# Two full seven-product sets per gate and up pair, a third running sum that stays a PSUM bank, and sums taken from turned tiles

## The chip, the cores and the metric

The kernel runs on one core of one Trainium2 chip. The metric is the device time of one execution in microseconds, the median of several runs. TensorE (PE) multiplies, VectorE (DVE) and ScalarE (ACT) prepare operands and empty PSUM, SyncE (SP) issues nearly all DMAs, GpSimd (POOL) does almost nothing here.

## What is computed

Two decoder layers on 256 rows of 2048 columns. In each layer a mixer (attention and a gated recurrence between an input and an output projection) is followed by a feed-forward part and a gate with input embeddings. The change lies in the feed-forward part and in a helper that other projections share:

```
h = rms_norm(x, pre_ffn_gain[i])
f = (silu(h @ w_ffn_gate[i]) * (h @ w_ffn_up[i])) @ w_ffn_down[i]
x = x + rms_norm(f, post_ffn_gain[i])
```

The gate and up weights are 2048 x 5632, the down weights 5632 x 2048, all fp32.

## The kernel before, in words

**Precision.** Every fp32 operand is split into two fp32r tiles, a rounded high part (a cast on ACT, line 203 or 305) and the rest (a subtraction on DVE, line 204 or 315). A product is then three matmuls: high by high, low by high, high by low.

**Tiles.** Rows come in two tiles of 128 (t = 0, 1). The inner dimension comes in chunks of 256, that is two slices k of 128. Weights come in tiles of 256 x 512 (`wr`, 512 KB, ten buffers; `wh` and `wl`, seven buffers each). One slice of one row tile against one weight tile is three matmuls of 512 columns, so a chunk costs 12 matmuls for both row tiles and one weight tile, and one split.

**strip (line 318)** multiplies all chunks plainly for one 512-column strip.

**paired (line 399)** does two strips, wa and wb, together. For two chunks it uses seven block products in place of eight (Strassen's scheme in Winograd's form, `fast`, lines 442 to 499). The left blocks are sums of row tiles (`mixed`, line 356), the right blocks sums and differences of weight tiles, made in place on DVE by `sub` (line 433), then split by `parts` (line 430). The products go into four running sums: u (first, sixth and seventh product; a bank of pool `pms`), `accc`, `acce`, `acca` (pool `pacc`, four banks). Three times u or `accc` is copied out by ACT (`saved`, line 425), and line 496 adds u to the copy of `accc` on DVE. The remaining chunks go through `plain` (line 503), wb's second row tile into a fresh bank `accd` (line 544 or 530). `second` (line 481) follows the first plain chunk of wa, `third` (line 487) follows the last. At the end of each sum, `summed` (line 392) or the caller's function adds bank and saved copy.

**Gate and up (gated, line 1178).** Eleven column strips in each layer; strip 0 goes plainly, strips 1 to 10 through `paired` with eight chunks: chunks 0 and 1 in seven products, and, by the argument `half`, chunk 2 cut into two slices of 128 and handled the same way (products of half the length; the sums from `mixed_half`, line 378). Chunks 3 to 7 are plain. Each finished strip is transposed through DRAM (`shuffled`, line 241: a DVE transpose, a store, four loads) and split into `hidden` (`split_shuffled`, line 279).

**Down.** The strips are consumed in groups of 2, 3, 3 and 3 (line 1208). Each group is multiplied with w_ffn_down, two output strips at a time, through `paired` with 4 or 6 chunks (the last group's output strips 2 and 3 plainly). The sums for this come from `mixed(first)`, over the group's first hidden strip, eight ticks into the group's last gate and up pair (line 1204).

**Order.** One counter of ticks (line 95) starts deferred steps (`later`, line 73). Engines run their own instruction lists in order; the order in a list is set by a scheduler in program order as far as its readiness estimate allows. All weight loads and all turn DMAs stand in SP's queue. `load_gain` (line 547) loads a broadcast gain row into one of two `gB` buffers.

Of the 40 calls of `paired` in the two layers, 4 belong to w_out, 20 to gate and up, 14 to down, 2 to the embedding gate (these with `after`).

Of the kernel before, what the change touches and what calls it, by code (L numbers as in the profile page):

```python
# [47 lines left out]
def decoder(ctx: ExitStack, tc: tile.TileContext, x, p, positions, w_in, attn_sinks,  # L48
# [307 lines left out]
    def mixed(lhs, tags=None):  # L356

        if tags:
# [19 lines left out]
    def mixed_half(x):  # L378

        hi = sp.tile([P, 4, 1, P], F32R, tag="ax", name="sum")  # L380
        lo = sp.tile([P, 4, 1, P], F32R, tag="ay", name="sum")
        full = nat((P, 2, SEQ))
        V.tensor_tensor(full, x[0][:, 0:2].bitcast(F32), x[1][:, 0:2].bitcast(F32), op=ALU.add)
        a11, a21, a12, a22 = (full[:, k, t * P:(t + 1) * P] for k in range(2) for t in range(NT))
        s = nat((P, 4, 1, P))
        for i, p, q, op in ((0, a21, a22, ALU.add), (1, s[:, 0, 0], a11, ALU.subtract),
                            (2, a11, a21, ALU.subtract), (3, a12, s[:, 1, 0], ALU.subtract)):
            V.tensor_tensor(s[:, i, 0], p, q, op=op)
        split(s, hi, lo)
        return lambda i: lambda k: (hi[:, i - 1, 0], lo[:, i - 1, 0])  # L390
# [8 lines left out]
    def paired(lhs, sums, wa, wb, cols, done_a, done_b, nch=8, row0=0, skews=(0, 0),  # L399
               after=None, mixed_order=False, half=None):  # L400
# [35 lines left out]
        def split_one(r, k):  # L436
            hi = wps.tile([P, 2, W], F32R, tag="wh", name="wh")
            lo = wps.tile([P, 2, W], F32R, tag="wl", name="wl")
            split(r[:, k], hi[:, k], lo[:, k])
            return hi, lo  # L440

        def fast():
            mix = sums()
            r11, r12 = fetch_w(wa, base, cols[0]), fetch_w(wb, base, cols[1])
            if half:
                more = half()
                g, p = fetch_w(wa, base + 2, cols[0]), fetch_w(wb, base + 2, cols[1])
            r21, r22 = fetch_w(wa, base + 1, cols[0]), fetch_w(wb, base + 1, cols[1])
            u = bank()
            acc(u, block(0, 0), parts(r11))  # L450
            if half:
                gx = parts(g)
                acc(u, block(2, 0), gx, (0,))
            x = [saved(u)]
            sub(r11, r12, r11)
            c = psum("accc")
            acc(c, mix(1), parts(r11))
            if half:
                sub(g[:, 0], p[:, 0], g[:, 0])
                acc(c, more(1), split_one(g, 0), (0,))  # L460
            p5 = saved(c)
            tick()
            e = psum("acce")
            acc(e, block(1, 0), parts(r21))
            if half:
                acc(e, block(2, 0), gx, (1,))
            sub(r11, r22, r11)
            sub(r21, r21, r11)
            a = psum("acca")
            acc(a, block(1, 1), parts(r21))  # L470
            if half:
                sub(g[:, 0], p[:, 1], g[:, 0])
                sub(g[:, 1], g[:, 1], g[:, 0])
                g24 = parts(g)
                acc(a, block(2, 1), g24, (1,))
                sub(p[:, 0], p[:, 1], p[:, 0])
            tick()
            sub(r12, r22, r12)
            y = []

            def second():
                acc(u, mix(2), parts(r11))
                if half:
                    acc(u, more(2), g24, (0,))
                y.append(saved(u))

            def third():
                acc(c, mix(4), parts(r22))
                if half:
                    p32 = parts(p)  # L490
                    acc(c, more(4), p32, (1,))
                acc(u, mix(3), parts(r12))
                if half:
                    acc(u, more(3), p32, (0,))
                x.append(saved(u))
                V.tensor_tensor(p5, u, p5, op=ALU.add)
                y.append(p5)
                tick()
            return e, a, c, x, y, second, third

        head = 3 if half else 2

        def plain(w, col, banks, skew, end, c0=head, c1=nch, then=None):
            n = c1 - c0
            ws = {}
            for i in range(n + skew):
                if i < n:
                    ws[i] = load_w(w, base + c0 + i, col)
                    acc(banks[0], block(c0 + i, 0), ws[i])
                    if i == n - 1 and end:  # L510
                        end(0)
                if i >= skew:
                    acc(banks[1], block(c0 + i - skew, 1), ws[i - skew])
# [6 lines left out]
        e, a, c, x1, x2, second, third = fast()  # L520
# [6 lines left out]
        if mixed_order:  # L527
            plain(wa, cols[0], (e, a), 0, None, c1=nch - 2, then=second)
            third()
            d = psum("accd")  # L530
            plain(wb, cols[1], (c, d), 0, None, c1=nch - 2)
            plain(wa, cols[0], (e, a), 0, end_a, c0=nch - 2)
            plain(wb, cols[1], (c, d), 0, end_b, c0=nch - 2)
# [10 lines left out]
        d = psum("accd")  # L544
# [205 lines left out]
    for l in range(DEPTH):  # L750
# [427 lines left out]
        def gated(n, last, first):  # L1178
            col = n * W
            gate = {}  # L1180

# [8 lines left out]
            def done_up(t, ps):  # L1190
                V.scalar_tensor_tensor(gate[t], ps, rx2(t)[:, 0:1], gate[t],
                                       op0=ALU.mult, op1=ALU.mult)
                d = shuffled(gate[t], slow=False)
# [141 lines left out]
```

## Time and profile before

| | |
|---|---|
| median of 3 runs | 2377.96 us (2377.86 to 2381.11) |
| profiled execution | 2380.66 us, span 2378.9 us, mean granted clock 0.998 |
| ACT busy | 1398.0 us (59%) |
| HBM | 212 GB/s over the span |
| one gate and up pair in steady state | 41.5 us, 183 matmuls of 512 columns |

The span is the time from the first to the last instruction that the profiler recorded. A row of the view of windows gives, for a stretch, each engine's busy time and the instructions that touch it. A row of the timeline gives start, length, engine, line, operation, out<-in and, in brackets, idle time of the engine just before it with what ended it. Matmuls are pipelined, so a matmul's length overlaps the next; what a matmul costs is the distance between starts.

### The profile page before, as it was taken

Reading aid. Unit: us, or ns where it says so; the run is one execution under the profiler, and the core shown is the slowest. Engines: PE = TensorE matmul, PEld = TensorE weight load, DVE = VectorE, ACT = ScalarE, POOL = GpSimd, SP = SyncE. Lnnn points to the kernel's source line nnn. Section 1 sums busy time; section 2 is a strip of 40 time slices with the busy share of each in tenths; the row PEclk is TensorE's granted clock in tenths of the full one; section 3 lists DMA queues with packets and bytes.
Section 4 is the critical chain, followed back from the end, with each engine's and each line's share of the span. In section 5 each row is a group of like instructions: output and inputs, shape, how many; then the busy total and the mean of one; then the engine's idle time right before and its main releaser. Section 6 shows DMA issues by size and latency. Waiting matters only on the chain.

```text
span 2378.9 us, 31721 instructions
## 1 busy us (share of the span) xinstructions
PE 2358.3 (99%) x10951; PEld 1950.6 (82%) x10951; DVE 2026.5 (85%) x2703; ACT 1398.0 (59%) x2000; POOL 106.6 (4%) x213
## 2 busy tenths in 40 slices
PE   9999999999999999999999999999999999999999
PEld 7888887887888888888788888878878888888887
DVE  7687987999999899888777879779999989998885
ACT  6565466556556555657556554665566565565564
POOL 3100001000000000001010000010000000000010
PEclk9999999999999999999999999999999999999999
DMA  8666467657566664766776663675765575667753
GB/s 290 216 187 203 151 199 250 223 199 244 181 226 219 241 230 166 272 220 203 227 222 207 184 209 132 226 257 180 241 219 193 206 254 198 230 209 251 243 169 133
DMA packets 301666, 506.05 MB, mean 213 GB/s; under 512 B 23712, under 2 KB 69696, under 8 KB 301504
## 3 DMA queue, kind: packets, MB, share of 16 engines
q1 hardware_dynamic: 301200, 503.93, 63.6%
q8 instruction: 86, 1.41, 0.2%
q14 instruction: 76, 0.62, 0.1%
q10 hardware_dynamic: 240, 0.07, 0.0%
q0 software_dynamic: 64, 0.02, 0.0%
HBM read 474.57 MB, written 29.36 MB: 212 GB/s over the span
## 4 chain that ended last, share of the span: by engine, by line
PE 92%; DVE 4%; issue 1%; DMA 1%; ACT 1%; POOL 1%; SPq 0%; DVEq 0%; ACTq 0%; POOLq 0%
PE acc L331 9%; PE acc L330 9%; PE acc L333 9%; PE accc L418 5%; PE accc L421 5%; PE accc L422 5%; PE acca L422 4%; PE acce L422 4%; PE acce L418 4%; PE acca L418 4%; PE acca L421 4%; PE acce L421 4%; PE accd L422 3%; PE accd L418 3%; PE accd L421 3%; PE ms L418 3%
## 5 line engine op out<-in xcount | busy, mean ns | idle before, releaser
L305 ACT CAST wh<-wr 128x1024 fp32r<-128x1024 f32 x980 | 1006.0, 1051 | 722.9 <-DVE wr L434 209.3
L315 DVE TENSOR_TENSOR wl<-wr,wh 128x1024 fp32r<-128x1024 f32 x980 | 1163.0, 1217 | 212.7 <-ACT wh L305 204.9
L330 PE MATMUL acc<-wh,ck 128*128 128x512 f32 x1056 | 417.5, 396 | 0.8 <-ACT ck L203 0.8
L331 PE MATMUL acc<-wh,ck 128*128 128x512 f32 x1056 | 413.4, 392 | 0.0
L333 PE MATMUL acc<-wl,ck 128*128 128x512 f32 x1056 | 412.2, 391 | 0.8 <-DVE wl L315 0.8
L434 DVE TENSOR_TENSOR wr<-wr 128x1024 f32<-128x1024 f32 (+1 forms) x240 | 243.8, 1038 | 0.8
L333 PEld LDWEIGHTS acc<-wl,ck 128*128 128x128 f32 x1056 | 198.7, 188 | 43.0 <-DVE wl L315 1.7
L331 PEld LDWEIGHTS acc<-wh,ck 128*128 128x128 f32 x1056 | 198.9, 188 | 40.3 <-DVE ck L204 0.4
L330 PEld LDWEIGHTS acc<-wh,ck 128*128 128x128 f32 x1056 | 198.5, 188 | 40.6 <-ACT ck L203 1.0
L418 PE MATMUL acca<-wh,ck 128*128 128x512 f32 x468 | 182.6, 390 | 3.1 <-ACT wh L305 3.1
L422 PE MATMUL acca<-wl,ck 128*128 128x512 f32 x468 | 182.3, 390 | 1.1 <-DVE wl L315 1.1
L418 PE MATMUL acce<-wh,ck 128*128 128x512 f32 x468 | 182.7, 390 | 0.4 <-ACT wh L305 0.4
L422 PE MATMUL acce<-wl,ck 128*128 128x512 f32 x468 | 182.3, 390 | 0.3 <-DVE wl L315 0.2
L421 PE MATMUL acce<-wh,ck 128*128 128x512 f32 x468 | 182.1, 389 | 0.0
L421 PE MATMUL acca<-wh,ck 128*128 128x512 f32 x468 | 182.1, 389 | 0.0
L422 PE MATMUL accd<-wl,ck 128*128 128x512 f32 x368 | 144.7, 393 | 0.0
L418 PE MATMUL accd<-wh,ck 128*128 128x512 f32 x368 | 143.7, 390 | 0.0
L421 PE MATMUL accd<-wh,ck 128*128 128x512 f32 x368 | 143.2, 389 | 0.0
L421 PE MATMUL accc<-wh,ck 128*128 128x512 f32 x368 | 143.2, 389 | 0.0
L422 PE MATMUL accc<-wl,ck 128*128 128x512 f32 x368 | 143.2, 389 | 0.0
L418 PE MATMUL accc<-wh,ck 128*128 128x512 f32 x368 | 143.1, 389 | 0.0
L418 PEld LDWEIGHTS acca<-wh,ck 128*128 128x128 f32 x468 | 87.8, 188 | 22.9 <-ACT wh L305 4.8
(277 smaller groups left out, 3362.2 us busy)
## 6 DMA issues: line engine op xcount, KB each, us to landing
wr<-in_w_in_dram SPq DMA_DIRECT2D x176, 512.0 KB, 4.9
wr<-in_w_ffn_gate_dram SPq DMA_DIRECT2D x176, 512.0 KB, 6.0
wr<-in_w_ffn_up_dram SPq DMA_DIRECT2D x176, 512.0 KB, 6.1
wr<-in_w_ffn_down_dram SPq DMA_DIRECT2D x176, 512.0 KB, 7.4
wr<-in_w_out_dram SPq DMA_DIRECT2D x64, 512.0 KB, 4.9
wr<-in_w_ple_gate_dram SPq DMA_DIRECT2D x64, 512.0 KB, 5.5
turn<-nat SPq DMA_DIRECT2D x86, 256.0 KB, 2.6
nat<-turn SPq DMA_DIRECT2D x344, 64.0 KB, 3.6
```

Source lines behind the costliest of these rows:

```text
L305: marks["hi"] = S.copy(hi, raw)
L315: marks["lo"] = V.tensor_tensor(lo, raw, hi.bitcast(F32), op=ALU.subtract)
L330: T.matmul(ps[t], xh, hi[:, k], start=first, stop=False)
L331: T.matmul(ps[t], xl, hi[:, k], start=False, stop=False)
L333: marks[t, c] = marks["pe"] = T.matmul(ps[t], xh, lo[:, k], start=False, stop=last)
L418: T.matmul(ps, xh, hi[:, k], start=id(ps) not in opened, stop=False, skip_group_check=True)
L421: T.matmul(ps, xl, hi[:, k], start=False, stop=False, skip_group_check=True)
L422: marks["pe"] = T.matmul(ps, xh, lo[:, k], start=False, stop=k == ks[-1], skip_group_check=True)
L434: V.tensor_tensor(dst, p, q, op=ALU.subtract)
```

## The change

1. `paired` takes `more` (a second full set of sums) in place of `half`, and `q`, the first chunk of the seven-product set. With `more`, chunks q, q+1 and q+2, q+3 go as two full sets of seven products, step by step in turn, into the same four running sums. Gate and up now have chunks 0 to 3 in products, 4 to 7 plain. `split_one` and `mixed_half` go.
2. The sum of line 496 goes: after the third save, u is not added to the copy of `accc` but goes on as the bank of wb's second row tile, in place of the fresh `accd`. With `after` (the embedding gate), u is taken from `pacc`.
3. Down's seven-product set is over chunks 2 and 3 of a group (q=2), the second hidden strip, and its sums come from the transposed fp32 tiles (`mixed_turned`), without adding high and low parts again. It is queued two ticks after that strip's split.
4. The second set of sums for gate and up is a full `mixed` whose tiles take the places of the old half set (`ax`, `ay`) and the two `gB` buffers.
5. The loads of the post-norm gain in the last group are queued three ticks later.

```diff
-    def mixed_half(x):
...
+    def mixed_turned(d):
+        out = [[nat((P, 2, 2, P), F32R) for i in range(2)] for _ in range(2)]
+        a = [[x[0][:, 2 * c:2 * c + 2] for x in d] for c in range(2)]
+        s = [nat((P, 2, 2, P)) for _ in range(2)]
+        s1, s2, s3, s4 = (quarters(s[i][:, j]) for i in range(2) for j in range(2))
+        for dst, p, q, op in ((s1, a[0][1], a[1][1], ALU.add), (s2, s1, a[0][0], ALU.subtract),
+                              (s3, a[0][0], a[0][1], ALU.subtract), (s4, a[1][0], s2, ALU.subtract)):
+            V.tensor_tensor(dst, p, q, op=op)
+        for i in range(2):
+            split(s[i], out[0][i], out[1][i])
...
         def fast():
+            quads = [(sums(), q)] + ([(more(), q + 2)] if more else [])
+            raw = [[fetch_w(w, base + c, col) for w, col in zip((wa, wb), cols)] for _, c in quads]
+            for r, (_, c) in zip(raw, quads):
+                r += [fetch_w(w, base + c + 1, col) for w, col in zip((wa, wb), cols)]
...
+            u = psum("accu") if after else bank()
+            each(lambda mix, c, r11, r12, r21, r22: acc(u, block(c, 0), parts(r11)))
             x = [saved(u)]
+            each(lambda mix, c, r11, r12, r21, r22: sub(r11, r12, r11))
+            cc = psum("accc")
+            each(lambda mix, c, r11, r12, r21, r22: acc(cc, mix(1), parts(r11)))
+            p5 = saved(cc)
             tick()
             e = psum("acce")
+            each(lambda mix, c, r11, r12, r21, r22: acc(e, block(c + 1, 0), parts(r21)))
+            if more:
+                tick()
+            def fourth(mix, c, r11, r12, r21, r22):
+                sub(r11, r22, r11)
+                sub(r21, r21, r11)
+            each(fourth)
             a = psum("acca")
+            each(lambda mix, c, r11, r12, r21, r22: acc(a, block(c + 1, 1), parts(r21)))
             tick()
+            each(lambda mix, c, r11, r12, r21, r22: sub(r12, r22, r12))
...
             def third():
+                each(lambda mix, c, r11, r12, r21, r22: acc(cc, mix(4), parts(r22)))
+                each(lambda mix, c, r11, r12, r21, r22: acc(u, mix(3), parts(r12)))
                 x.append(saved(u))
-                V.tensor_tensor(p5, u, p5, op=ALU.add)
                 y.append(p5)
                 tick()
-            return e, a, c, x, y, second, third
+            return e, a, cc, u, x, y, second, third
...
-        e, a, c, x1, x2, second, third = fast()
+        e, a, c, d, x1, x2, second, third = fast()
...
-            d = psum("accd")
...
-            if last:
-                later(8, lambda: hx.append(mixed(first)))
             paired(xT, lambda: sx[0], w_ffn_gate[l], w_ffn_up[l], (col, col), summed(done_gate),
-                   summed(done_up), half=lambda: sx[1])
+                   summed(done_up), more=lambda: sx[1])
```

More of the change, by code (lines that the diff above doesn't have):

```diff
@@ L376, in mixed @@
         return lambda i: lambda k: tuple(a[(i - 1) // 2][:, (i - 1) % 2, k] for a in out)
-    def mixed_half(x):
[L380 to L390, printed above, removed]
+    def mixed_turned(d):
[8 more added lines that the diff above has]
+            split(s[i], out[0][i], out[1][i])
+        return lambda i: lambda k: tuple(a[(i - 1) // 2][:, (i - 1) % 2, k] for a in out)
     def summed(done):
@@ L399, in paired @@
     def paired(lhs, sums, wa, wb, cols, done_a, done_b, nch=8, row0=0, skews=(0, 0),
-               after=None, mixed_order=False, half=None):
+               after=None, mixed_order=False, more=None, q=0):
         base = row0 // (2 * P)
@@ L434, in sub, with each @@
             V.tensor_tensor(dst, p, q, op=ALU.subtract)
[L436 to L440, printed above, removed]
-        def fast():
[L443 to L453, printed above, removed]
-            x = [saved(u)]
[L455 to L461, printed above, removed]
+        def fast():
+            quads = [(sums(), q)] + ([(more(), q + 2)] if more else [])
+            raw = [[fetch_w(w, base + c, col) for w, col in zip((wa, wb), cols)] for _, c in quads]
+            for r, (_, c) in zip(raw, quads):
+                r += [fetch_w(w, base + c + 1, col) for w, col in zip((wa, wb), cols)]
+            def each(fn):
+                for (mix, c), r in zip(quads, raw):
+                    fn(mix, c, *r)
+            u = psum("accu") if after else bank()
+            each(lambda mix, c, r11, r12, r21, r22: acc(u, block(c, 0), parts(r11)))
+            x = [saved(u)]
+            each(lambda mix, c, r11, r12, r21, r22: sub(r11, r12, r11))
+            cc = psum("accc")
+            each(lambda mix, c, r11, r12, r21, r22: acc(cc, mix(1), parts(r11)))
+            p5 = saved(cc)
@@ L495, in third, with plain @@
                 x.append(saved(u))
-                V.tensor_tensor(p5, u, p5, op=ALU.add)
                 y.append(p5)
                 tick()
-            return e, a, c, x, y, second, third
-        head = 3 if half else 2
-        def plain(w, col, banks, skew, end, c0=head, c1=nch, then=None):
-            n = c1 - c0
+            return e, a, cc, u, x, y, second, third
+        rest = [i for i in range(nch) if not q <= i < q + (4 if more else 2)]
+        def plain(w, col, banks, skew, end, cs=rest, then=None):
+            n = len(cs)
@@ L512, in plain @@
                 if i >= skew:
[L513 removed]
+                    acc(banks[1], block(cs[i - skew], 1), ws[i - skew])
                 if then and i == 0:
@@ L1176, in decoder, with gated @@
         sx = []
-        def gated(n, last, first):
+        def gated(n, last, quad):
             col = n * W
             gate = {}
+            turned = []
             def done_gate(t, ps):
@@ L1193, in done_up @@
                 d = shuffled(gate[t], slow=False)
+                turned.append(d)
                 later(wait, lambda: split_shuffled(d, None, hl, t))
+                if quad and t == 1:
+                    later(wait + 2, lambda: hx.append(mixed_turned(turned)))
             if n == 0:
@@ L1198, in gated @@
                 sx.append(mixed(xT[0], ("kv", "at")))
-                sx.append(mixed_half(xT[1]))
+                sx.append(mixed(xT[1], homes=[
+                    [sp.tile([P, 2, 2, P], F32R, tag=g, name="sum") for g in ("ax", "ay")],
+                    [np_.tile([P, 2, 2, P], F32R, tag="gB", name="sum", bufs=2) for i in range(2)]]))
                 later(4, lambda: sx.append(leave_x()))
```

54 lines of the change are left out of this document (17 added, 37 removed).

## The prediction

> **What bounds the kernel now.** I read the page's busy times first, then the chain that ended last, then the view of windows over single pairs of the feed-forward part, where the change is.
>
> ```profile
> span 2378.9 us, 31721 instructions
> PE 2358.3 (99%) x10951; PEld 1950.6 (82%) x10951; DVE 2026.5 (85%) x2703; ACT 1398.0 (59%) x2000; POOL 106.6 (4%) x213
> ...
> PEclk9999999999999999999999999999999999999999
> ...
> PE 92%; DVE 4%; issue 1%; DMA 1%; ACT 1%; POOL 1%; SPq 0%; DVEq 0%; ACTq 0%; POOLq 0%
> ```
>
> PE is busy nearly always, its clock is granted in full, and 92% of the chain runs through it. A pipelined engine's busy time can hide waiting, so I look at a stage whose matmuls I can count. The windows show two steady gate and up pairs (from the first product of one to that of the next), a group's two down pairs, and the first group's two down pairs; columns are length, then PE, PEld, DVE, ACT, POOL busy.
>
> ```profile
> 754.10:795.60 41.50, 41.50 (x184) 34.36 (x184) 37.52 (x41) 25.43 (x30) 0.00 (x0) 1.00 0.68 228
> 795.60:837.10 41.50, 41.50 (x184) 34.35 (x183) 37.61 (x44) 24.15 (x30) 0.00 (x0) 1.00 0.66 228
> 837.10:868.70 31.60, 31.60 (x139) 25.66 (x138) 30.34 (x33) 18.45 (x22) 0.00 (x0) 1.00 0.71 233
> 868.70:900.00 31.30, 31.30 (x140) 25.90 (x138) 29.61 (x32) 18.11 (x21) 0.00 (x0) 1.00 0.56 202
> 521.90:543.20 21.30, 21.30 (x95) 17.28 (x94) 21.27 (x25) 13.83 (x17) 0.00 (x0) 1.00 0.76 230
> 543.20:565.00 21.80, 20.28 (x89) 16.17 (x88) 20.37 (x22) 12.89 (x15) 0.00 (x0) 1.00 0.60 209
> ```
>
> By the code a gate and up pair has 183 matmuls of 512 columns (the 184 counts one already running): 63 in products, 120 plain. 41.50 / 183 = 0.2268 us each, and PE never idles in these rows. So the pair is PE's. DVE is close behind: 37.6 of 41.5 us, 30.3 of 31.6, and in the first group's down pairs 21.27 of 21.30.
>
> **The change part by part.**
>
> *Matmuls.* Before, one full set saves 6 matmuls and the half set 3 of the plain 192. After, two full sets save 12: 84 in products, 96 plain, 180 in all. Three fewer in 20 pairs are 60; 60 x 0.2268 = **13.6 us off PE**. No other matmul count changes: `q` moves which chunks form the set, not how many.
>
> *DVE work.* These rows price an operation: five splits of 1024 columns in a run, and the distance between two neighbours of 512.
>
> ```profile
> 760.28 5.72 DVE L315 TENSOR_TENSOR wl<-wr,wh 128x1024 fp32r<-128x1024 f32 x5
> ...
> 784.79 1.22 DVE L315 TENSOR_TENSOR wl<-wr,wh 128x1024 fp32r<-128x1024 f32 x1
> 785.92 2.95 DVE L434 TENSOR_TENSOR wr<-wr 128x1024 f32<-128x1024 f32 x3
> ...
> 794.54 0.68 DVE L395 TENSOR_TENSOR nat<-accc,nat 128x512 f32<-128x512 f32 x1
> 795.14 0.68 DVE L434 TENSOR_TENSOR wr<-wr 128x512 f32<-128x512 f32 x1
> ```
>
> A 1024-column operation costs 5.72 / 5 = 1.14 us, a 512-column one 795.14 - 794.54 = 0.60. A pair's splits go from 20 full and one half to 22 full (14 in products, 8 plain): 2 x 1.14 - 0.60 = +1.68. Its weight sums go from 4 full and 4 half to 8 full: 4 x (1.14 - 0.60) = +2.16. The dropped line 496 gives back 0.60. Net +3.24, so the two pairs above would need 40.8 and 40.9 us of DVE against 180 x 0.2268 = 40.8 of PE. That is the crux: **the slack of 3.9 us a pair is spent to nothing.** Relief stands beside it:
>
> ```profile
> L496 DVE TENSOR_TENSOR nat<-ms,nat 128x512 f32<-128x512 f32 x40 | 27.4, 684 | 3.7 <-ACT nat L427 3.7
> L367 DVE TENSOR_TENSOR nat<-ck 128x512 f32<-128x512 f32 x28 | 18.7, 681 | 0.0
> ```
>
> The 20 calls outside gate and up lose line 496 too, and each of the eight groups' `mixed_turned` loses two of line 367's additions (1.2 us). A steady group of three gate and up pairs and two down pairs spends 171.14 us of DVE in 187.30; it goes to 171.14 + 3 x 3.24 - 2 x 0.60 - 1.20 = 178.5, in 187.30 - 9 x 0.2268 = 185.3 of PE, 96%.
>
> ```profile
> 712.70:900.00 187.30, 187.30 (x827) 154.57 (x825) 171.14 (x185) 110.82 (x127) 0.00 (x0) 1.00 0.64 219
> ```
>
> Down pairs already run at 30.34 / 31.60 = 96% without a PE stall, so 96% can be carried if DVE starts each product phase far enough ahead. At 784.79 the split, and behind it the weight sums (line 434, used only in products), are for the pair that starts at 795.60: a store of about 10.8 us. What the head of a pair draws from it (the first four steps, u to `acca`): before, 36 matmuls, 8.2 us, against six splits and a half (7.4) and three full and three half sums (5.2); after, 48 matmuls, 10.9 us, against eight splits (9.1) and six sums (6.8). The draw grows from 4.4 to 5.0, and on both sides some 3.7 us come on top for emptying the pair before (six operations of 512 columns). 8.7 of 10.8: it holds, narrowly. From below it costs 0; from above, DVE's whole idle time of 41.50 - 37.52 = 4.0 us a pair stays and each pair becomes 44.8 long, 20 x 3.3 = +66. I take 0.05 us a pair, **+1**, near the lower end because the down rows are the nearest case.
>
> *The Trainium skill on this.* The page "Perfetto Trace Analysis", section "Identifying the Most-Contended Engine", says that the most contended engine is the one with the highest occupancy, that matmul busy time doesn't count for this, and that TensorE's headroom is judged by weight-load busy time (or MFU). By that rule VectorE, at 85% against 82% of weight loads, is the engine to relieve, and a change that loads it more runs slower. The trace speaks against it so far: matmuls that start every 0.2268 us through whole pairs leave nothing to gain elsewhere. What it would make of the time is a rival below.
>
> *First group.* Here DVE has already run out, once in the second down pair and again at the head of the next gate and up pair:
>
> ```profile
> 546.36 0.39 PE L422 MATMUL acce<-wl,ck 128*128 128x512 f32 x1
> 548.04 0.50 PE L418 MATMUL acca<-wh,ck 128*128 128x512 f32 x1 [1.30 <-ACT wh L305]
> ...
> 570.88 0.39 PE L422 MATMUL acce<-wl,ck 128*128 128x512 f32 x1
> 571.52 0.50 PE L418 MATMUL acca<-wh,ck 128*128 128x512 f32 x1 [0.25 <-ACT wh L305]
> 571.85 0.40 PE L421 MATMUL acca<-wh,ck 128*128 128x512 f32 x1
> 572.78 0.50 PE L422 MATMUL acca<-wl,ck 128*128 128x512 f32 x1 [0.53 <-DVE wl L315]
> ```
>
> Starts late by 1.45, 0.41 and 0.70 us: about 2.6 a layer. The groups' down pairs get 2 x 0.60 + 1.20 = 2.4 lighter, the next head draws 0.6 more, and the pair before enters with less rest. Bounds: all 2.6 gone, or doubled, in two layers: -5 to +5. I take 0.
>
> *The new wait.* u now goes on as a bank, so wb's second row tile may write it only after ACT's third copy has read it. Before, it had a fresh bank. Behind that wait stands everything on PE. The rows are the last u matmul, the first `accd` matmul and the copy, in a gate and up pair and in a w_out pair:
>
> ```profile
> 823.28 0.39 PE L422 MATMUL ms<-wl,sum 128*128 128x512 f32 x1
> 824.87 0.39 PE L418 MATMUL accd<-wh,ck 128*128 128x512 f32 x1
> ...
> 822.84 1.05 ACT L305 CAST wh<-wr 128x1024 fp32r<-128x1024 f32 x1 [0.79 <-ACT wh L305]
> 823.80 0.58 ACT L427 COPY nat<-ms 128x512 f32<-128x512 f32 x1
> ...
> 330.88 0.39 PE L422 MATMUL ms<-wl,sum 128*128 128x512 f32 x1
> 332.47 0.39 PE L418 MATMUL accd<-wh,ck 128*128 128x512 f32 x1
> ...
> 332.09 0.58 ACT L427 COPY nat<-ms 128x512 f32<-128x512 f32 x1
> ```
>
> PE leaves 1.59 us between them (six matmuls on `accc`). In the first case the copy, behind a cast, ends at 824.38, 0.49 early; in the second at 332.67, 0.20 late. A cast of 1.05 us that starts just ahead of the copy makes it late. From below 0; from above the copy waits a whole cast in all 40 calls: about 0.5 x 40 = 20. Taken: most calls as in the first row, a few as in the second, **+1**.
>
> *Embedding gate.* u moves to the four `pacc` banks, so `acca` now needs the bank that the strip before still holds until its second sigmoid has read it. In layer 0:
>
> ```profile
> 1149.21 0.67 ACT L1273 ACTIVATE nat<-acc,rp 128x512 f32<-128x512 f32 x1
> ...
> 1147.32 0.39 PE L418 MATMUL acca<-wh,ck 128*128 128x512 f32 x1
> ...
> 1156.07 0.80 PE L418 MATMUL ms<-wh,sum 128*128 128x512 f32 x1 [2.25 <-ACT nat L427]
> ```
>
> The sigmoid ends at 1149.88, 2.6 us after `acca` started. But PE stands 2.25 us a little later anyway, for a copy that doesn't hang on it; the wait moves forward rather than adds. -2 to +3; taken 0.
>
> *At nothing.* The full second `mixed` adds, once a layer, one addition and one split of 512 columns (1.2 us) and makes four sums twice as long (an estimated 0.4 us more), during strip 0's up; if nothing covered it, 1.6 us a layer. The weight loads of a pair's head are eight in place of six of ten buffers, so chunks 6 and 7 of gate wait for a buffer, freed by the `acca` splits about 10 us before their turn; a load lands in 6.0:
>
> ```profile
> wr<-in_w_ffn_gate_dram SPq DMA_DIRECT2D x176, 512.0 KB, 6.0
> ```
>
> The gain loads move behind that head in SP's queue and are read only when the pair's first sum is done; if they were late, DVE would wait a landing, once a layer.
>
> **Sum:** -13.6 + 1 + 1 = -11.6. The profiled execution took 2380.66 us, 2.7 above the median 2377.96; it would become 2369.1, and the median **2366.4**.
>
> **The rivals.**
>
> *Stalls vanish as well.* If the lighter down pairs and the dropped line 496 take the first group's waits away and nothing new appears: -13.6 - 5, about 2359 to 2362. For it: line 496 blocks DVE in order behind an ACT copy (3.7 us idle). Against: the heads grow. Chance 0.08.
>
> *The new wait decides.* The third copy stands behind a cast in most of the 40 calls, 0.15 to 0.3 us each, 6 to 12 us: 2370 to 2376. For it: the w_out row. Against: only a 0.49 us margin must hold. 0.14, half of it still faster.
>
> *DVE becomes the bound (slower).* The place is the gate and up pair; the mechanism is that the DVE waits on ACT's casts remain when its work fills the pair:
>
> ```profile
> L315 DVE TENSOR_TENSOR wl<-wr,wh 128x1024 fp32r<-128x1024 f32 x20 | 23.7, 1218 | 4.0 <-ACT wh L305 3.7 <-PE ms L422 0.3
> ```
>
> A pair is then 40.8 plus what remains of these 4.0. It decides from 0.7 us on (41.5 - 40.8). With 2 us left, 42.8: 20 x 1.3 = +26, **2404**; with 1 us, 2384. For it: zero slack. Against: those waits lie in the pair's plain part, where all seven `wl` buffers are full and DVE can't run ahead; they should shrink when DVE is short. Over the whole kernel DVE gains 20 x 3.84 - 40 x 0.60 - 8 x 1.20 + 2 x 1.6 = 46 us, so 2424 is its end. The skill's rule above comes out here. Chance 0.18: 0.12 slower, 0.06 with under 0.7 us left, within 0.2%.
>
> **How the numbers follow.** My forecast (2362 to 2370) has 0.60. About 0.2%, 4.8 us, is what a measurement of this kernel can tell from no change. Faster: 0.60 + 0.08 + 0.07 = 0.75; same: 0.07 + 0.06 = 0.13; slower 0.12. The range runs from 2360, the stall-free case, to 2378, over the whole new-wait case and the mild DVE one; the slower rival stays out.
>
> **What would show it.** Right: 60 matmuls fewer; steady pairs 40.8 us long; DVE over 95% in them with PE starts still 0.2268 apart; line 305 waiting less on PE's buffers. The new wait would show as PE idle ahead of an `ms` matmul after the third copy (released by line 427); DVE's bound as PE idle released by lines 305 or 315 at `acce`, `acca` or the first plain chunk of every pair, with pairs over 41.5 us. That last would make the prediction wrong.

## The result and the profile after

After 2383.64 us median (2380.5 to 2387.29, 15 runs), before 2378.61 us beside it (2377.13 to 2381.11, 15 runs): a ratio of 1.002, interval 1.0012 to 1.0028. The change makes the kernel a little slower, where 2366.4 and "faster" was predicted, and the time lies outside the range.

The page of after, with the busy times and the chain:

```profile
span 2384.4 us, 31615 instructions
...
PE 2351.7 (99%) x10891; PEld 1939.8 (81%) x10891; DVE 2072.3 (87%) x2671; ACT 1421.3 (60%) x2022; POOL 104.2 (4%) x213
...
PE 82%; DVE 11%; issue 3%; DMA 2%; ACT 1%; POOL 1%; SPq 0%; DVEq 0%; ACTq 0%; POOLq 0%
```

The 60 matmuls are gone (10951 - 10891). The chain tells where their time went: PE's share falls from 92% to 82%, DVE's rises from 4% to 11%. The windows of after over single pairs (columns as before: length, then PE, PEld, DVE, ACT, POOL) show it stage by stage: the first gate and up pair behind the first group's down, then, of a steady group, the three gate and up pairs and the first down pair, and last that group as a whole (three gate and up pairs and two down pairs).

```profile
563.52:608.63 45.11, 42.97 (x182) 34.76 (x180) 41.86 (x39) 26.61 (x29) 0.00 (x0) 0.96 0.52 187
...
714.18:754.98 40.80, 40.80 (x182) 33.78 (x181) 38.45 (x37) 25.59 (x28) 0.00 (x0) 1.00 0.57 207
754.98:796.44 41.46, 41.11 (x181) 33.71 (x180) 40.66 (x41) 26.50 (x30) 0.00 (x0) 1.00 0.66 228
796.44:836.55 40.11, 39.76 (x176) 32.58 (x174) 37.27 (x42) 23.91 (x29) 0.00 (x0) 1.00 0.69 236
836.55:870.34 33.79, 32.17 (x140) 25.59 (x139) 33.10 (x35) 21.07 (x24) 0.00 (x0) 1.00 0.66 218
...
714.18:902.98 188.80, 186.47 (x818) 152.68 (x817) 178.44 (x181) 114.71 (x130) 0.00 (x0) 1.00 0.63 218
```

Of the three gate and up pairs only the first is 40.80 us long with PE full throughout. In the second, PE is short by 0.35 us of busy time and the pair is as long as one before with three matmuls more. The third window holds only 174 of its pair's 180 matmuls: the last six write the bank of u (`ms`), as the next pair's first product does right behind them, and fall into the next window. It too is 0.66 us over 174 x 0.2267 = 39.45. The window of the first down pair (which in turn leaves its own last six to the next) is 33.79 us, where 138 matmuls take 31.3. The group takes 188.80 us; it took 187.30 before, and 185.3 was expected.

What PE waited for in after and in before (engine, what, line, releaser: us in total, times, longest):

```profile
PE acca L423 <- DVE wl L315: 5.8, 11, 0.9
PE ms L419 <- ACT nat L428: 3.7, 6, 1.1
PE acce L422 <- DVE ck L204: 2.7, 5, 1.1
PE acce L419 <- ACT wh L305: 2.7, 2, 1.3
```

```profile
PE acca L418 <- ACT wh L305: 3.1, 4, 1.3
PE ms L418 <- ACT nat L427: 2.2, 1, 2.2
PE acca L422 <- DVE wl L315: 1.1, 2, 0.5
```

Two kinds have grown or are new: at `acca`, for a weight split on DVE (the head of gate and up pairs), and at `ms` and `acce` in the down pairs, for a copy of u and for the split of the last hidden strip. (Line numbers in `paired` are one higher in after: 419, 422, 423 are the three matmuls, 428 is the copy in `saved`, 435 is `sub`.) Adding up what every distance between matmul starts has in excess of 0.227 us, over both layers, gives the account, after less before: first gate and up pair of the second group +5.1 us, the other gate and up pairs +8.9, the six down pairs with a mixed order (output strips 0 and 1 of each group of three strips, where the chunks of the last hidden strip come last) +7.6, the first group's down -1.8, the embedding gate -1.8. That is +18.0 against -13.6 of matmuls: +4.4 of the 5.5 between the two spans. The row of before for the first of these, against 45.11 us above:

```profile
564.99:608.27 43.28, 42.36 (x184) 34.11 (x183) 39.94 (x42) 26.39 (x30) 0.00 (x0) 1.00 0.55 195
```

**The head of a gate and up pair.** The timeline of after around the pair that starts at 796.44, first the pair's first split on DVE, its weight sums and the splits for `acca`, then the `acca` matmuls:

```profile
783.95 1.23 DVE L315 TENSOR_TENSOR wl<-wr,wh 128x1024 fp32r<-128x1024 f32 x1
785.21 1.23 DVE L435 TENSOR_TENSOR wr<-wr 128x1024 f32<-128x1024 f32 x1
...
788.09 1.22 DVE L435 TENSOR_TENSOR wr<-wr 128x1024 f32<-128x1024 f32 x1
...
790.35 1.22 DVE L435 TENSOR_TENSOR wr<-wr 128x1024 f32<-128x1024 f32 x1
...
793.76 1.22 DVE L435 TENSOR_TENSOR wr<-wr 128x1024 f32<-128x1024 f32 x1
...
799.20 3.45 DVE L435 TENSOR_TENSOR wr<-wr 128x1024 f32<-128x1024 f32 x3
...
803.20 1.18 DVE L435 TENSOR_TENSOR wr<-wr 128x1024 f32<-128x1024 f32 x1
804.30 7.03 DVE L315 TENSOR_TENSOR wl<-wr,wh 128x1024 fp32r<-128x1024 f32 x6
...
804.83 0.39 PE L422 MATMUL acca<-wh,ck 128*128 128x512 f32 x1
805.57 0.50 PE L423 MATMUL acca<-wl,ck 128*128 128x512 f32 x1 [0.35 <-DVE wl L315]
```

All eight sums of the pair stand on DVE ahead of the first `acca` split, which starts behind the last of them, at 804.30. The matmul that needs it, the 39th of the pair, is due at 804.83 + 0.23 and starts 0.5 us late. From 785.21 to the end of that split (805.44) DVE never idles: eight sums and six splits at 1.14 us, seven operations of 512 columns at some 0.62. With the split at 783.95 that is 21.5 us of DVE from the pair's first split to the one that `acca` waits for. DVE starts 12.5 us ahead of the pair (783.95 to 796.44), and the pair has 38 matmuls, 8.6 us, ahead of the one that waits: together 0.4 us too little.

DVE's issue list, the order in which the built program has DVE run its instructions, names the tiles of the eight (the first figure counts the entries). In this pair r11, r12, r21, r22 are `wr` 7267, 7269, 7275, 7277 for the first set and 7271, 7273, 7279, 7281 for the second:

```
891 L435 TENSOR_TENSOR wr_7267<-wr_7269,wr_7267 128x1024
894 L435 TENSOR_TENSOR wr_7271<-wr_7273,wr_7271 128x1024
896 L435 TENSOR_TENSOR wr_7269<-wr_7277,wr_7269 128x1024
899 L435 TENSOR_TENSOR wr_7267<-wr_7277,wr_7267 128x1024
906 L435 TENSOR_TENSOR wr_7275<-wr_7275,wr_7267 128x1024
907 L435 TENSOR_TENSOR wr_7271<-wr_7281,wr_7271 128x1024
908 L435 TENSOR_TENSOR wr_7273<-wr_7281,wr_7273 128x1024
910 L435 TENSOR_TENSOR wr_7279<-wr_7279,wr_7271 128x1024
911 L315 TENSOR_TENSOR wl_7359<-wr_7275,wh_7357 128x1024
```

896 and 908 are r22 - r12, which only `third` uses, at the end of wa's strip. In the program they come behind the `acca` product; the list has them ahead of its splits.

**The first down pair.** The timeline of after: ACT, and PE at the place where it stands.

```profile
838.78 7.69 ACT L305 CAST wh<-wr 128x1024 fp32r<-128x1024 f32 x8 [5.17 <-DVE wr L435]
846.84 1.06 ACT L305 CAST wh<-wr 128x1024 fp32r<-128x1024 f32 x1 [0.36 <-PE acca L422]
848.33 0.62 ACT L203 CAST ck<-nat 128x512 fp32r<-128x512 f32 x1 [0.44 <-DMA nat<-turn]
849.58 1.05 ACT L305 CAST wh<-wr 128x1024 fp32r<-128x1024 f32 x1 [0.62 <-PE acca L422]
850.53 0.58 ACT L428 COPY nat<-ms 128x512 f32<-128x512 f32 x1
...
851.11 0.50 PE L422 MATMUL acce<-wh,ck 128*128 128x512 f32 x1 [1.12 <-DVE ck L204]
851.45 0.40 PE L419 MATMUL ms<-wh,nat 128*128 128x512 f32 x1
```

The copy at 850.53 is the first save of u, of a product whose last matmul started at 839.04. It stands behind ten weight casts and a cast of hidden, and the second product on u (`ms<-wh,nat`) writes the bank that the copy reads, so it starts behind it, at 851.45. PE has nothing else to do: `acce` and `acca` are down to the hidden strip that is just being split, and wb's second row tile now goes into u itself. Before, in the same pair, the copy was nearly as late (11.8 us behind the pair's first matmul, 12.6 after), but PE had that row tile's matmuls for the fresh `accd`:

```profile
848.91 0.58 ACT L427 COPY nat<-ms 128x512 f32<-128x512 f32 x1
...
847.99 0.39 PE L418 MATMUL accd<-wh,ck 128*128 128x512 f32 x1
...
850.70 0.40 PE L418 MATMUL ms<-wh,nat 128*128 128x512 f32 x1
```

**The first group's down pairs.** Here the wait that the prediction had feared does come, once in each layer: wb's second row tile, now in u, waits for ACT's third copy, which ends at 539.75 behind two weight casts and a cast of hidden. In layer 0:

```profile
539.81 0.50 PE L419 MATMUL ms<-wh,ck 128*128 128x512 f32 x1 [1.07 <-ACT nat L428]
```

The matmul starts 1.23 us late. These two are 2.1 of the 3.7 us at `ms` above.

### The profile page after: what moved, and what is told of

Read it like the earlier page. It is cut to its first block, busy times and chain, and to the rows that moved or that the text cites. A ratio compares the mean times of both kernels' runs of the same rounds, so it can differ in the third digit from the quotient of the medians.

```text
span 2384.4 us, 31615 instructions
## 1 busy us (share of the span) xinstructions
PE 2351.7 (99%) x10891; PEld 1939.8 (81%) x10891; DVE 2072.3 (87%) x2671; ACT 1421.3 (60%) x2022; POOL 104.2 (4%) x213
## 4 chain that ended last, share of the span: by engine, by line
PE 82%; DVE 11%; issue 3%; DMA 2%; ACT 1%; POOL 1%; SPq 0%; DVEq 0%; ACTq 0%; POOLq 0%
PE acc L330 9%; PE acc L331 9%; PE acc L333 9%; PE ms L419 5%; PE ms L423 5%; PE ms L422 5%; PE accc L423 4%; PE accc L422 4%; PE accc L419 4%; PE acca L423 4%; PE acca L419 4%; PE acca L422 4%; DVE wl L315 3%; PE acce L423 3%; PE acce L419 3%; PE acce L422 3%
## 5 line engine op out<-in xcount | busy, mean ns | idle before, releaser
L305 ACT CAST wh<-wr 128x1024 fp32r<-128x1024 f32 x1020 | 1039.0, 1052 | 699.6 <-DVE wr L435 222.2
L315 DVE TENSOR_TENSOR wl<-wr,wh 128x1024 fp32r<-128x1024 f32 x1020 | 1209.7, 1220 | 178.5 <-ACT wh L305 174.1
L435 DVE TENSOR_TENSOR wr<-wr 128x1024 f32<-128x1024 f32 x240 | 285.4, 1217 | 1.1
L419 PE MATMUL acca<-wh,ck 128*128 128x512 f32 x448 | 176.2, 393 | 2.3 <-ACT wh L305 1.6
L422 PE MATMUL acce<-wh,ck 128*128 128x512 f32 x448 | 175.0, 391 | 2.9 <-DVE ck L204 2.7
L419 PE MATMUL acce<-wh,ck 128*128 128x512 f32 x448 | 174.9, 390 | 2.7 <-ACT wh L305 2.7
L422 PE MATMUL acca<-wh,ck 128*128 128x512 f32 x448 | 175.6, 392 | 0.0
L419 PE MATMUL ms<-wh,ck 128*128 128x512 f32 x420 | 164.7, 392 | 2.1 <-ACT nat L428 2.1
L422 PE MATMUL ms<-wh,ck 128*128 128x512 f32 x420 | 163.5, 389 | 0.0
L423 PE MATMUL ms<-wl,ck 128*128 128x512 f32 x420 | 163.2, 389 | 0.0
L422 PE MATMUL accc<-wh,ck 128*128 128x512 f32 x328 | 127.6, 389 | 0.0
L423 PE MATMUL accc<-wl,ck 128*128 128x512 f32 x328 | 127.6, 389 | 0.0
L419 PE MATMUL accc<-wh,ck 128*128 128x512 f32 x328 | 127.6, 389 | 0.0
L423 PEld LDWEIGHTS acca<-wl,ck 128*128 128x128 f32 x448 | 84.8, 189 | 29.5 <-DVE wl L315 11.5
```

Of the source, the lines that this page charges most:

```text
L305: marks["hi"] = S.copy(hi, raw)
L315: marks["lo"] = V.tensor_tensor(lo, raw, hi.bitcast(F32), op=ALU.subtract)
L419: T.matmul(ps, xh, hi[:, k], start=id(ps) not in opened, stop=False, skip_group_check=True)
L422: T.matmul(ps, xl, hi[:, k], start=False, stop=False, skip_group_check=True)
L423: marks["pe"] = T.matmul(ps, xh, lo[:, k], start=False, stop=k == ks[-1], skip_group_check=True)
L435: V.tensor_tensor(dst, p, q, op=ALU.subtract)
```

## The experiments

Ratios are to the kernel before, run on the same chip, with 95% intervals; each time is a median. The theory was: DVE misses the deadline at the head of the gate and up pairs, and u as a bank takes cover away in the down pairs. The rivals: DVE's work as a whole is the bound, or the third copy's wait is.

**1. u as the bank alone.** In the kernel before, item 2 of the change and nothing else.

```diff
-            u = bank()
+            u = psum("accu") if after else bank()
...
-                V.tensor_tensor(p5, u, p5, op=ALU.add)
-        d = psum("accd")
-        e, a, c, x1, x2, second, third = fast()
+        e, a, c, d, x1, x2, second, third = fast()
```

> The kernel before with one part alone: the third running sum goes on as the bank of the second strip's row tile 1 (no addition of line 496, no fresh bank; in the embedding gate u lies in pacc). Gate and up keep the full and the half set. DVE theory (the two full sets fill DVE, and PE waits for its splits): this part only takes 24 us off DVE, so 2375 to 2379, no new waits in gate and up. Wait theory (PE waits for ACT's third copy before it may write the bank): 2382 to 2385, PE idle before ms matmuls released by the copy.

2382.01 us, ratio 1.0014 (1.0005 to 1.0023). Its first down pair in the windows, and its waits at `ms`:

```profile
836.77:869.59 32.82, 32.15 (x140) 25.66 (x138) 31.25 (x33) 21.00 (x24) 0.00 (x0) 1.00 0.68 225
```

```profile
PE ms L418 <- ACT nat L427: 5.6, 8, 1.1
```

It takes 40 DVE operations away (24 us of DVE) and is slower all the same: the down pair goes from 31.61 to 32.82. The time is where the wait theory had put it, but six of the eight waits are for the first copy, in the six down pairs with a mixed order. The other two, 2.1 us in all, are for the third copy in the first group's down pairs. Gate and up pairs have no wait; there the third copy costs nothing.

**2. The full set without the bank.** After, with u summed into the copy as before and a fresh `accd`.

```diff
+                V.tensor_tensor(p5, u, p5, op=ALU.add)
...
+            d = psum("accd")
...
+        d = psum("accd")
```

> The changed kernel with the third sum as before: line 496's addition and a fresh bank. DVE theory: 24 us of DVE work more, so slower than the changed kernel, 2386 to 2393. Wait theory: the new wait is gone, 2366 to 2376.

2379.73 us, ratio 0.9999 (0.999 to 1.0008), between the two expectations: the bank did cost time, but its going leaves the loss at the heads. The down pairs are back at 31.65 us, but gate and up pairs are 40.80, 41.39 and 41.6: what remains of the change still loses its 13.6 us at the heads.

**3. The half set back.** After, with before's half set in gate and up in place of the second full one.

```diff
-                   summed(done_up), more=lambda: sx[1])
+                   summed(done_up), half=lambda: sx[1])
...
-        e, a, c, d, x1, x2, second, third = fast()
+        e, a, c, d, x1, x2, second, third = halves() if half else fast()
```

> The changed kernel with the half set of before in gate and up, all else as changed (third sum as bank, seven products over the group's second hidden strip, sums of turned tiles, later gain loads). DVE theory: 2373 to 2379, the waits for splits at acca in gate and up gone. Theory that the new order or the turned sums in down cost the time: 2382 to 2386, with the waits for ck in down still there. Wait theory: 2382 to 2385.

2397.43 us, ratio 1.0077 (1.0065 to 1.009).

```profile
PE acce L433 <- ACT ck L203: 8.6, 6, 1.4
PE ms L437 <- DVE wl L315: 4.0, 2, 2.0
PE acce L436 <- DVE ck L204: 3.2, 6, 0.5
```

Gate and up pairs are free of waits (41.48 us with 183 matmuls); all the loss is in the down pairs, 34.1 to 35.6 us, where PE stands for the split of the last hidden strip. So the second full set isn't what hurts the down pairs: without it the bank costs more. The time lies above all three expected ranges, and why the bank costs so much more here was not followed up.

**4. The turned sums alone.** Before, with items 3 and 5 only (q=2, `mixed_turned`, the later gain loads).

```diff
-            if last:
-                later(8, lambda: hx.append(mixed(first)))
+                if quad and t == 1:
+                    later(wait + 2, lambda: hx.append(mixed_turned(turned)))
...
-                           mixed_order=s == 1 and glen > 2)
+                           mixed_order=s == 1 and glen > 2, q=2)
```

> The kernel before with the down part alone: the seven-product set over the second hidden strip of a group, its sums from the turned tiles, queued two ticks after that strip's split, the gain loads later. Half set in gate and up, fresh bank and line 496 as before. If this part is neutral or helps (two additions less a group on DVE): 2374 to 2379. If it costs by itself (PE asks for the last hidden strip earlier): 2382 to 2392, with waits at acce for ck.

2376.71 us, ratio 0.9987 (0.9979 to 0.9996): a small gain, as the lighter DVE would have it.

**5. DVE made heavier.** Before, with three of a gate and up pair's splits (those for `accc`, `acce` and `acca` of the first set) done twice, 3.4 us of DVE more in a pair, as much as the change adds. The second split writes the same values.

```diff
+            if again:
+                V.tensor_tensor(hl[1], r, hl[0].bitcast(F32), op=ALU.subtract)
...
-            acc(c, mix(1), parts(r11))
+            acc(c, mix(1), parts(r11, half))
...
```

> The kernel before, with three splits of each gate and up pair subtracted twice on DVE (same result, 3.4 us more DVE work a pair, in the head; no matmul changed). DVE theory: a pair then needs about 41 us of DVE in 41.5 of PE, and the same waits as in the changed kernel come up at acca and at ck: 8 to 18 us more, 2387 to 2397. Wait theory and order theory: none of their parts is in it, so no more than 2 us more, up to 2381.

2427.37 us, ratio 1.0203 (1.0189 to 1.0217). A pair in the windows, and the two largest waits:

```profile
764.64:808.64 44.00, 42.60 (x184) 34.03 (x183) 40.91 (x44) 24.65 (x29) 0.00 (x0) 1.00 0.62 215
```

```profile
PE acca L418 <- ACT wh L305: 17.4, 15, 1.3
PE acce L418 <- ACT wh L305: 5.6, 18, 1.2
```

68 us of DVE work cost 49 us of time, far above the 8 to 18 expected, though DVE has only 40.9 us to do in pairs of 44.0. Put at the head, about seven tenths of the work's length is lost; the pair's idle DVE time takes up little of it.

**6. The fresh bank in the down pairs only.** After, with the sum and the fresh `accd` back in the six down pairs with a mixed order.

```diff
+                if mixed_order:
+                    V.tensor_tensor(p5, u, p5, op=ALU.add)
...
+            d = psum("accd")
```

> The changed kernel, but in the down pairs written in mixed order (output strips 0 and 1 of the groups of three) the third sum is added on DVE and wb's row tile 1 gets a fresh bank, as before; gate and up and all other pairs keep u as the bank. Theory of order (the wait for the third copy makes the scheduler put products of the last hidden strip ahead of the third sum, and PE then stands for that strip's split): the waits at acce for ck and at ms for the second copy, 1.4 to 2.3 us in each of six groups, go: 2371 to 2379. Theory of the plain wait (ACT's copy itself is late in every pair): most pairs keep it, 2381 to 2385.

2375.55 us, ratio 0.9988 (0.9979 to 0.9996): 8 us below after.

**7. The last differences on GpSimd.** The kernel of 6, with r22 - r12 of both sets (896 and 908 above) on GpSimd.

```diff
-            each(lambda mix, c, r11, r12, r21, r22: sub(r12, r22, r12))
+            each(lambda mix, c, r11, r12, r21, r22: (G if more else V).tensor_tensor(
+                r12, r22, r12, op=ALU.subtract))
```

> As fresh_in_down, and the last weight difference of both sets in gate and up (r22 minus r12, two of eight a pair) on GpSimd: 2.3 us a pair less on DVE, same matmuls. DVE theory: the waits for line 315's splits and line 305's casts at acca in gate and up go, 6 to 12 us below fresh_in_down, 2362 to 2371. Rival (the work's amount on DVE is not it, the chain sub, cast, split is): within 2 us of fresh_in_down, or slower where GpSimd's sums come too late for the third step.

2419.43 us, ratio 1.0167 (1.0153 to 1.0181). This was meant to free DVE and did the opposite. The timeline, GpSimd and then DVE beside it:

```profile
798.04 3.17 POOL L466 TENSOR_TENSOR wr<-wr 128x1024 f32<-128x1024 f32 x1 [35.25 <-DMA wr<-in_w_ffn_gate_dram]
802.51 3.18 POOL L466 TENSOR_TENSOR wr<-wr 128x1024 f32<-128x1024 f32 x1 [1.30 <-issue]
...
799.47 2.83 DVE L435 TENSOR_TENSOR wr<-wr 128x1024 f32<-128x1024 f32 x1
802.22 4.55 DVE L315 TENSOR_TENSOR wl<-wr,wh 128x1024 fp32r<-128x1024 f32 x2
806.69 1.21 DVE L435 TENSOR_TENSOR wr<-wr 128x1024 f32<-128x1024 f32 x1
```

While GpSimd adds, DVE's operations take about twice as long: 2.83 against 1.21 us for the same sum. So this run says nothing of the theory; it is no way to lighten DVE.

**8. One plain chunk ahead of `acca`.** The kernel of 6, with gate's first plain chunk multiplied between the `acce` and the `acca` product. DVE's work is the same.

```diff
+            a = psum("acca")
+            if more:
+                hl = load_w(wa, base + rest[0], cols[0])
+                acc(e, block(rest[0], 0), hl)
+                acc(a, block(rest[0], 1), hl)
             each(fourth)
-            a = psum("acca")
...
```

> As fresh_in_down, and in gate and up the first plain chunk of gate goes ahead of the acca product of both sets: same work on every engine, but DVE gets 12 matmuls (2.7 us) more for one split before it owes the acca splits. DVE theory in the form 'the head of a pair asks too early': 3 to 8 us below fresh_in_down. In the form 'a pair's DVE work as a whole fills the pair': within 2 us of it, the waits come up later in the pair.

2359.76 us, ratio 0.9921 (0.9908 to 0.9935), the best version found; it beats both kernels. It is 15.8 us below the kernel of 6, about twice the 3 to 8 expected. The busy times of its page, then the windows of the first pair behind the first group's down and of a second gate and up pair of a group:

```profile
PE 2339.2 (99%) x10891; PEld 1938.8 (82%) x10891; DVE 2073.0 (88%) x2677; ACT 1424.2 (60%) x2022; POOL 104.0 (4%) x213
```

```profile
561.38:603.31 41.93, 41.10 (x182) 33.71 (x181) 41.55 (x39) 26.33 (x29) 0.00 (x0) 1.00 0.56 201
...
747.57:788.37 40.80, 40.80 (x182) 33.78 (x181) 40.44 (x41) 26.46 (x30) 0.00 (x0) 1.00 0.67 232
```

40.44 us of DVE fit into 40.80 with PE full. Twelve matmuls give the `acca` split 2.7 us more, for 1.14 us of one split more ahead of it, and the wait of 0.5 us is gone. DVE's work as a whole is therefore not the bound.

**9. The last differences left out.** The kernel of 6 without r22 - r12 in gate and up.

```diff
-            each(lambda mix, c, r11, r12, r21, r22: sub(r12, r22, r12))
+            if not more:
+                each(lambda mix, c, r11, r12, r21, r22: sub(r12, r22, r12))
```

> fresh_in_down with part of the computation left out: the last weight difference of both sets in gate and up (two of eight sums a pair) isn't made, 2.3 us a pair less on DVE and nothing more anywhere. DVE theory, amount: the waits at acca in gate and up go, 2360 to 2368. If only the place in the head counts (these sums come after the acca splits in program order): 2371 to 2376.

2359.73 us, ratio 0.9919 (0.9905 to 0.9932). The same time as 8: no wait in steady gate and up pairs. Taking away the two sums that stand early in the list does as much as moving the deadline. The expectation meant to tell the amount of work from its place, but it took these sums to come behind the `acca` splits; as the list has them ahead, this run alone can't tell the two apart, and 8, with the work unchanged, does. A list with the same two sums moved behind the splits was not run.

**10. The plain chunk with the bank kept.** After, with the edit of 8 alone.

> The changed kernel with one thing alone: the first plain chunk of gate ahead of the acca product (u stays the bank in all pairs). If the two causes add, 16 us below the changed kernel: 2365 to 2370, with the waits at acce for ck and at ms for the second copy left in the down pairs. If the down waits came only from DVE being late out of gate and up, they go as well: 2358 to 2363.

2369.18 us, ratio 0.9956 (0.9944 to 0.9969). With 6 and 8 this makes a square:

| | u the bank in mixed down pairs | fresh bank there |
|---|---|---|
| `acca` straight after `acce` | 2383.64 (after) | 2375.55 |
| a plain chunk between | 2369.18 | 2359.76 |

The head is worth 14.5 and 15.8 us, the bank 8.1 and 9.4. The two causes add, and they are near the account above (14.0 and 7.6).

**11. The bank only in gate and up and w_out.** The kernel of 8, with a fresh bank in all down pairs and in the embedding gate.

```diff
+                if not keep:
+                    V.tensor_tensor(p5, u, p5, op=ALU.add)
...
+        if not keep:
+            d = psum("accd")
```

> As plain_ahead, with u as the bank only in gate and up and in w_out; all down pairs and the embedding gate have a fresh bank and line 496's addition. The waits at ms for the copy in the first group (1.2 us twice) and at acca for the sigmoid (2.2 us) go; 16 additions of 0.6 us come back on DVE. Theory of order: 2353 to 2359. If those pairs gain from the lighter DVE: 2360 to 2364.

2360.73 us, ratio 0.9926 (0.9913 to 0.9938): no better than 8, as the second expectation had it. The two waits for the third copy in the first group go, but two at `acca` for ACT's casts come there (1.7 us in all). Of the embedding gate's waits one goes and another comes back (`ms` for ACT's copy, 1.9 us).

**12. The order on PE held.** A theory of mine for the down pairs: PE's list puts the products of the just finished hidden strip too far ahead. After, with those matmuls kept behind the ones that precede them in the program.

```diff
-            plain(wa, cols[0], (e, a), 0, end_a, cs=rest[-2:])
+            with behind("pe"):
+                plain(wa, cols[0], (e, a), 0, end_a, cs=rest[-2:])
```

> The changed kernel with the matmuls of the last hidden strip into gate's sums held behind those of the second strip's first chunks (program order) in the mixed-order down pairs; u stays the bank everywhere. Theory of order: PE no longer stands at acce for ck, and only the wait for the third copy is left, under 0.3 us a pair: 2373 to 2379. Rival, the bank's wait itself: 2381 to 2386, the idle time moves to ms.

2387.76 us, ratio 1.0035 (1.0023 to 1.0048). The theory falls: the waits at `acce` for the hidden strip's split go, and at least as much time is lost at `ms` (the time lies a little above both expected ranges).

```profile
PE ms L419 <- ACT nat L428: 10.6, 8, 1.5
```

In the six down pairs with a mixed order it is the late first copy that PE waits for, whatever is ahead of it.

**13 and 14. Another buffer for the first copy.** Why is it late? Supposed: none of the 12 `nat` buffers is free for it when ACT's list is laid out. Both runs keep u as the bank and write that one copy, in the six down pairs, to the single tile `junk`; 13 is after, 14 is the kernel of 10.

```diff
-            x = [saved(u)]
+            x = [saved(u, np_.tile([P, W], F32, tag="junk", name="junk", bufs=1)
+                       if mixed_order else None)]
...
```

> The kernel after, with one edit: in the mixed-order down pairs the first copy of u goes to the single `junk` tile in place of a `nat` buffer; u stays the bank. The issue list of ScalarE puts that copy behind three weight casts, where the kernel after has it behind ten and a cast of hidden. If the lack of a free `nat` buffer makes the copy late and that makes TensorE stand in the down pairs, the waits at `ms` for line 428 and at `acce` for line 204 go in those pairs, a down pair is 31.7 us again, and the time falls by 7 to 9 us to about 2375 to 2377, as with the fresh bank there. If something else holds the down pairs (the copy of `accc`, the split of the last hidden strip, DVE's load), the wait moves to another releaser and the time stays at 2381 to 2386. The gate and up waits at `acca` stay in both cases.

> The same edit of the first copy on top of the kernel with the plain chunk ahead of the `acca` product (u the bank everywhere, 2369.18 before). If the missing buffer is the cause of the down pairs' waits, 2359 to 2362, as with the fresh bank in the down pairs, and no wait of more than 1 us at `ms` in the down pairs but for the first group's. If not, 2367 to 2370.

13: 2379.44 us, ratio 1.0002 (0.9993 to 1.0011), between the two expectations: about half of the bank's cost goes. 14: 2361.63 us, ratio 0.9929 (0.9916 to 0.9941), where the buffer theory had put it, 7.5 us below the kernel of 10. The timeline and the windows of 14:

```profile
828.11 2.95 ACT L305 CAST wh<-wr 128x1024 fp32r<-128x1024 f32 x3 [2.85 <-DVE wr L435]
830.96 0.57 ACT L428 COPY junk<-ms 128x512 f32<-128x512 f32 x1
```

```profile
827.73:859.30 31.57, 31.57 (x140) 25.75 (x138) 29.49 (x32) 18.79 (x22) 0.00 (x0) 1.00 0.71 234
```

With a buffer of its own the copy stands behind three casts of the pair's head instead of ten, and the down pair is 31.57 us long with u as the bank. In 13 the waits at `ms` in these six pairs go too, but those at `acce` for DVE's split of hidden (line 204) stay, 2.2 us in 5, and those at `acca`: there DVE enters the down pair late from the gate and up pairs. That this is all of the other half wasn't tried by itself.

## Why the prediction was wrong

**Matmuls: right.** 60 fewer, and where nothing waits, 40.80 / 180 = 0.2267 us each. Experiments 8 and 9 show that the whole 13.6 us was there to be had, and more.

**DVE's work: right.** 178.44 us in the steady group, 178.5 predicted; over the kernel 2072.3 - 2026.5 = 45.8, predicted 46.

**The store: the step that failed.** "8.7 of 10.8: it holds, narrowly", taken at +1. It doesn't hold: the heads cost 8.9 us, with a wait of 0.3 to 1.1 us in twelve pairs, all but the first of each group. The step counted six sums ahead of `acca`, as the program orders them. DVE's list has eight there, and the two more are 2.28 us, more than the margin of 2.1. In before the list had it so too: the last of the three sums at 785.92 is already r22 - r12. The step also set its work against all 48 matmuls of the head, but the first `acca` split is due after 38 of them. By after's own rows the head asks for 21.5 - 8.6 = 12.9 us ahead of the pair, where DVE starts 12.5 ahead. Experiment 9 takes these two out, 8 moves the deadline by 2.7 us, and both remove the waits; 5 puts work at this place and loses.

**The first group: "0", with bounds of -5 to +5.** Its down pairs gained 1.8 us: the waits for casts at `acca` went, 2.3 us a layer with what follows them, and the wait for the third copy came. But the pair behind them lost 5.1 (43.28 to 45.11 twice, and three matmuls fewer): net +3.3, inside the bounds. In experiment 8 that pair is 41.93 us, so most of its loss too hangs on the deadline.

**The new wait: priced in the wrong place.** "+1" was for wb's second row tile behind ACT's third copy. That wait isn't seen in gate and up; it comes once a layer in the first group's down pairs, 1.23 us each, 2.5 in all, which is in the account of that group. What the step missed is what the fresh `accd` did besides: its matmuls filled PE's time in the down pairs while the first copy was late. The bank costs 7.6 us there by the account, 8.1 and 9.4 by the square. A buffer of its own moves the copy forward and takes that cost away, shown by 14.

**The embedding gate: nearly right.** The wait moved from `ms` to `acca` and `accu` and shrank by 1.8, taken as 0 within -2 to +3.

**The rivals.** "Stalls vanish as well", 2359 to 2362, is what the change gives once both causes are mended (8: 2359.76). Its condition, that nothing new appears, did not hold in the change itself. "DVE becomes the bound" had the right place and named the right wait to look for, but not the mechanism: it reckoned with the waits on ACT's casts and a pair as long as DVE's work plus those. DVE had room in the pair; it was late at one point of it. Its case of 1 us left gives 2384, the time measured, but by luck: it has every pair 41.8 us long, where the longest steady ones are 41.5, and the down pairs make up the rest. Over the 18 pairs that don't follow the first group's down, 8.9 us are 0.5 a pair, under the 0.7 from which that rival decided. It takes back most of the 0.68 us that three matmuls give, and the pair behind the first group and the down pairs make the kernel slower.

The rule of the Trainium skill, page "Perfetto Trace Analysis", section "Identifying the Most-Contended Engine", as the prediction applied it, would have had the more loaded DVE make the kernel slower, and it did. But the kernel of 8 has DVE at 88% and is 0.8% faster than the one before with 85%: the occupancy gave the right sign here for another reason than load.

## What to carry to other kernels

When one engine's work is to fill another's time to the last tenth, don't add up a stage: write down, for the first consumer that can run out, everything that the producer's issue list has ahead of it, from the list and not from the program's order. Before a buffer is saved by reusing it, look at which work only the extra buffer let run early, and what it was covering. If the sums say that the work fits and the trace says that it waits, move other work ahead of the deadline (here twelve matmuls, 14 to 16 us) before giving up the change.

## What the runs showed of the hardware

**GpSimd slows DVE.** A 128x1024 fp32 sum took 3.2 us on GpSimd, and DVE's sum of the same shape beside it 2.83 instead of 1.21 us (experiment 7): 40 sums moved off DVE, 45.6 us at 1.14, cost 44 us of time. The Trainium skill, page "GPSIMD Engine Reference", section "Key points", says that GpSimd shares its SBUF interfaces with VectorE and contends with DVE instructions that have two SBUF inputs; the trace agrees, and this is the size of it.

**A wait of PE can cost more than itself.** The windows of after behind the two waits of the first group's next pair (the granted clock is the figure ahead of the last two):

```profile
571.50:575.70 4.20, 2.06 (x7) 1.11 (x6) 4.20 (x4) 4.07 (x5) 0.00 (x0) 0.95 0.00 0
575.70:578.50 2.80, 2.80 (x8) 2.21 (x7) 2.80 (x4) 1.81 (x3) 0.00 (x0) 0.50 0.81 252
```

Behind 2.5 us of waiting within some 3.1, the clock granted to PE was 0.50 for 2.8 us: matmuls started every 0.427 us, some 1.4 us lost on top. In experiment 3 the same followed on 2.4 us (1.59 and 0.82 close together) in the down pairs; the single waits of 1.56 us in experiment 12 had no such tail (1.00 behind the one at 849.96), while before's single wait of 2.25 us at 1156.07 had one (0.50 over the next 3.2 us).
